# Every engine's instructions in the order of the framework's finer simulation in place of its simple one

## The chip, the cores and the metric

The kernel runs on one core of a Trainium2 chip. A core has five engines with a queue of instructions each: TensorE (PE, matrix products), VectorE (DVE), ScalarE (ACT), GpSimd (POOL) and SyncE (SP, which here only issues transfers). An engine takes its instructions in the order in which they stand in its queue, and they wait for each other across engines by semaphores. The metric is the device time of one execution in microseconds, as a median of runs.

## The reference, cut to what matters

Two networks of two layers each, one behind the other, on 512 tokens of width 1024, in float32. The first also has 256 context tokens:

```
first_block:  per layer
  h = modulate(rms_norm(x), shift, scale)     # from c: w_mod, w_ada
  a = mla_attend(...)       # 8 heads, latent queries and keys
  b = diff_attend(...)      # 4 heads: softmax(q1 k1) - lam * softmax(q2 k2)
  x = x + gate * (merge of a and b) @ w_out
  x = x + gate * conv_ffn(modulate(rms_norm(x)))      # hidden width 2816
second_block:  per layer
  m = even_mixer(rms_norm(x))   # layer 0: pooling and a gated unit
  m = odd_mixer(rms_norm(x))    # layer 1: sparse attention (compressed,
                                #   selected, window keys) and retention
  x = x + rms_norm(m)
  x = x + rms_norm(swiglu(rms_norm(x)))
```

## The kernel before, in words

Activations lie with the 1024 features on partitions, as eight tiles of 128 x tokens (512, or 768 with the context). Every float32 weight tile of 128 x 1024 is loaded by SP into `wraw` (L286), and split into a high part `whi` (ACT, L295) and the rest `wlo` (DVE, L296). Activations `u` are split the same way (L319 to L324). A product is three matmuls: high by high, high by low, low by high (`mm` L330, `prods` L425). There are three buffers each for `wraw`, `whi` and `wlo`.

A norm runs over several engines: squares on ACT (L496), sums of tiles on DVE or POOL (L498), column sums on PE (L509, L586), scale and epsilon on DVE (L342), the power -1/2 on POOL (L343), and a broadcast over partitions on PE (`rowcast`, L349). What uses the broadcast differs by place: L1431/L1433 at startup, L1247/L1250 in the first network, L1604/L1605 and L324 in the second.

The modulation vectors of a layer come from 32 blocks of `w_ada` (`araw`, 512 KB each, L524). For each block and each of the two conditions DVE multiplies and sums (L537) and adds a bias (L538):

```
nc.vector.tensor_scalar(v[:, :n], sums, scale, eps, ...)           # L342
nc.gpsimd.tensor_tensor(r, v[:, :n], self.mhalf[:, :n], op=ALU.pow) # L343
nc.vector.scalar_tensor_tensor(self.junk, raw, 0.5, self.silu[cnd],
                       op0=ALU.mult, op1=ALU.mult, accum_out=m)     # L537
```

In the differential heads a score unit is four matmuls into one `psJ` (L751); its maximum is DVE's L778, its exponential ACT's L769. Then PE transposes the probabilities (L684) and multiplies them by the values. In the sparse attention, keys and values of blocks are summed into compressed ones: DVE builds `cmpx` (L1914), ACT and DVE split it into `cmpp` (L1918, L1919), PE multiplies it by the compression weights (L1927).

Two things set the order. The code issues work interleaved by hand: `weave` (L1048) and `beside` (L435) step several generators by pace numbers in the table `W`, and `ahead_by` raises the priority of some instructions. Then the framework's scheduler, in the `TileContext` of L2410, simulates the engines and puts on each engine's queue, in turn, the instruction that is ready and has the highest priority in that simulation. Priorities follow the order of the code.

## Time and profile before

| | us |
|---|---|
| median of three runs | 3378.22 |
| range | 3376.92 to 3384.22 |
| the profiled execution | 3375.24 |
| its span | 3373.4 |
| PE busy in it | 3266.5 (97%) |
| DVE busy | 2249.4 (67%) |
| ACT busy | 1386.3 (41%) |
| POOL busy | 491.6 (15%) |

Busy is the time in which an engine has an instruction in work; a PE that is busy can still run at the lower of its two clocks. The chain of work that ended last is PE for 45% of the span, DVE 4%, ACT 2% and POOL 1%. TensorE's granted clock is 0.8 to 0.9 of full speed in the first of the 40 slices and near full behind it.

### The profile page before, as it was taken

What the parts mean: (1) busy time and instruction counts of PE and PEld (TensorE: products, weight loads), DVE (VectorE), ACT (ScalarE), POOL (GpSimd) and SP (SyncE); (2) the same over time, 40 slices, a digit from 0 to 9 for tenths busy, and PEclk for the clock granted to TensorE, in tenths of its full rate; (3) what the DMA queues carried; (4) which work ended last, traced back from release to release, by engine and by line L of the source; (5) the groups of instructions that cost most, each with busy time, mean ns of one, the idle gap of its engine ahead of it and who ended that gap; (6) DMA issues with size and microseconds to landing.
All of it is one profiled execution on the core that took longest, in us unless ns stands there. A gap on an engine that the chain in (4) does not pass through costs nothing.

```text
span 3373.4 us, 45291 instructions
## 1 busy us (share of the span) xinstructions
PE 3266.5 (97%) x17605; PEld 2777.2 (82%) x17605; DVE 2249.4 (67%) x3822; ACT 1386.3 (41%) x2389; POOL 491.6 (15%) x490
## 2 busy tenths in 40 slices
PE   7999999999999999998999999999999989999998
PEld 4888878888888887887788888888888877798887
DVE  7958788468775565667866656777555777764555
ACT  5236566233222243545734333454232435552222
POOL 2002133210000011112330000221000513420001
PEclk8999999999999999999999999999999999999999
DMA  8721113323442121221162223222323231222222
GB/s 301 261 80 34 54 35 114 130 74 126 162 163 88 63 100 60 91 75 35 48 210 82 96 98 106 77 97 79 103 94 112 84 105 45 91 94 88 95 99 75
DMA packets 106567, 339.43 MB, mean 101 GB/s; under 512 B 12592, under 2 KB 18096, under 8 KB 106352
## 3 DMA queue, kind: packets, MB, share of 16 engines
q1 hardware_dynamic: 97920, 314.38, 27.8%
q0 software_dynamic: 3248, 11.67, 0.9%
q10 hardware_dynamic: 5184, 10.49, 0.8%
q8 instruction: 138, 2.26, 0.3%
q14 instruction: 77, 0.63, 0.1%
HBM read 312.24 MB, written 24.25 MB: 100 GB/s over the span
## 4 chain that ended last, share of the span: by engine, by line
PE 45%; DVE 4%; ACT 2%; issue 2%; POOL 1%; DMA 0%; ACTq 0%; POOLq 0%; DVEq 0%; SPq 0%
PE psM L425 38%; PE psM L330 2%; PE psJ L974 1%; DVE u L324 1%; PE psM L1032 1%; PE psM L2125 1%; PE psM L2086 1%; DVE wlo L296 0%; PE psM L684 0%; DVE t L1605 0%; PE psM L2117 0%; DVE t L1604 0%; PE psM L509 0%; POOL sm L343 0%; POOL stat L498 0%
## 5 line engine op out<-in xcount | busy, mean ns | idle before, releaser
L425 PE MATMUL psM<-u,whi 128*128 128x512 f32 (+1 forms) x5312 | 1434.6, 362 | 2.5 <-ACT u L322 1.0
L425 PEld LDWEIGHTS psM<-u,whi 128*128 128x128 f32 x5312 | 928.0, 189 | 157.3 <-ACT u L322 2.4
L425 PE MATMUL psM<-u,wlo 128*128 128x512 f32 (+1 forms) x2656 | 912.9, 362 | 1.9 <-DVE wlo L296 1.9
L295 ACT ACTIVATE whi<-wraw 128x1024 fp32r<-128x1024 f32 x393 | 413.6, 1054 | 990.0 <-PE psM L425 609.9
L296 DVE TENSOR_TENSOR wlo<-wraw,whi 128x1024 fp32r<-128x1024 f32 x393 | 488.4, 1244 | 279.8 <-ACT whi L295 277.7
L425 PEld LDWEIGHTS psM<-u,wlo 128*128 128x128 f32 x2656 | 481.3, 189 | 78.8 <-DVE wlo L296 2.6
L330 PE MATMUL psM<-u,whi 128*128 128x512 f32 (+1 forms) x1610 | 428.7, 352 | 2.7 <-DVE u L320 1.3
L330 PEld LDWEIGHTS psM<-u,whi 128*128 128x128 f32 x1610 | 280.2, 190 | 45.0 <-issue 2.1
L330 PE MATMUL psM<-u,wlo 128*128 128x512 f32 (+1 forms) x805 | 280.4, 349 | 0.0
L425 PE MATMUL psM<-u,wspare 128*128 128x256 f32 (+1 forms) x1584 | 254.7, 315 | 4.3 <-DVE t L1604 3.2
L425 PE MATMUL psJ<-u,whi 128*128 128x512 f32 (+1 forms) x1184 | 257.6, 337 | 0.0
L425 PEld LDWEIGHTS psM<-u,wspare 128*128 128x128 f32 x1584 | 225.0, 194 | 21.4 <-issue 3.3
L498 POOL TENSOR_TENSOR stat<-stat,t 128x256 f32<-128x256 f32 x100 | 94.7, 961 | 973.3 <-ACT t L496 907.6
L425 PEld LDWEIGHTS psJ<-u,whi 128*128 128x128 f32 x1184 | 181.8, 188 | 27.1
L330 PEld LDWEIGHTS psM<-u,wlo 128*128 128x128 f32 x805 | 152.8, 190 | 20.2 <-DVE wlo L296 0.4
L537 DVE SCALAR_TENSOR_TENSOR silu<-araw,silu 128x1024 f32<-128x1024 f32 x128 | 156.0, 1219 | 16.6 <-DMA araw<-in_w_ada_dram 16.4
L322 ACT ACTIVATE u<-t 128x512 fp32r<-128x512 f32 (+2 forms) x114 | 77.5, 682 | 215.1 <-DVE t L1308 128.3
L425 PE MATMUL psJ<-u,wlo 128*128 128x512 f32 x592 | 154.2, 338 | 0.0
L320 DVE TENSOR_TENSOR pt<-psM,pt 128x512 fp32r<-128x512 f32 x156 | 105.9, 685 | 36.9 <-ACT pt L319 35.3
L319 ACT ACTIVATE pt<-psM 128x512 fp32r<-128x512 f32 x156 | 91.5, 595 | 88.9 <-PE psM L684 83.2
L324 DVE SCALAR_TENSOR_TENSOR u<-t,u 128x512 fp32r<-128x512 f32 (+2 forms) x114 | 88.1, 775 | 49.3 <-ACT u L322 49.2
L330 PE MATMUL psM<-whi,u 128*128 128x512 f32 (+2 forms) x356 | 113.0, 386 | 4.0 <-DVE V L655 2.6
(356 smaller groups left out, 4385.2 us busy)
## 6 DMA issues: line engine op xcount, KB each, us to landing
wraw<-in_w_up_dram SPq DMA_DIRECT2D x88, 512.0 KB, 3.5
wraw<-in_ffn_gu_dram SPq DMA_DIRECT2D x88, 512.0 KB, 3.5
araw<-in_w_ada_dram SPq DMA_DIRECT2D x80, 512.0 KB, 4.3
wraw<-in_w_in_dram SPq DMA_DIRECT2D x70, 512.0 KB, 3.5
wraw<-in_w_down_dram SPq DMA_DIRECT2D x44, 512.0 KB, 3.5
wraw<-in_ffn_dn_dram SPq DMA_DIRECT2D x44, 512.0 KB, 3.5
wraw<-in_od_in_dram SPq DMA_DIRECT2D x24, 512.0 KB, 3.5
araw<-in_w_mod_dram SPq DMA_DIRECT2D x16, 512.0 KB, 10.2
```

Source lines behind the costliest of these rows:

```text
L295: nc.scalar.activation(hi[:, :n], raw[:, :n], AF.Copy)
L296: (nc.gpsimd if pool else nc.vector).tensor_sub(lo[:, :n], raw[:, :n], hi[:, :n].bitcast(F32))
L319: nc.scalar.activation(hi, src, AF.Copy)
L320: (nc.gpsimd if pool else nc.vector).tensor_sub(lo, src, hi.bitcast(F32))
L322: nc.scalar.activation(hi, src, AF.Copy, scale=scale) if isinstance(scale, float) else \
L324: nc.vector.scalar_tensor_tensor(lo, src, scale, hi.bitcast(F32), op0=ALU.mult, op1=ALU.subtract)
L330: nc.tensor.matmul(out, w[a][wrows, wcols], x[b][xrows, xcols], start=first and i == 0, stop=last and i == 2)
L425: self.nc.tensor.matmul(ps[:, lo - c0:hi - c0], w[a][:, wc], x[b][:, lo:hi], start=first and i == 0 and a == b, stop=last and i == len(ks) ...
L498: (nc.vector if last == 1 else nc.gpsimd).tensor_add(st["acc"][:, c], st["acc"][:, c], s[:, c])
L537: nc.vector.scalar_tensor_tensor(self.junk, raw, 0.5, self.silu[cnd], op0=ALU.mult, op1=ALU.mult, accum_out=m)
L974: self.nc.tensor.matmul(ps[:, c0 - keys[0][0]:c1 - keys[0][0]], q[:96, x, qs:qs + 128], k[:96, y, c0:c1], start=i == 0, stop=i == 2)
L1032: nc.tensor.matmul(o, V[:, kt, i], pt[:, b], start=kt == 0 and b == 0, stop=kt == 5 and b == 1)
```

## The change

One argument of the context in which the whole kernel is built. With it the scheduler runs its simulation of the engines in the finer form instead of the simple one. The instructions, their tiles and their number stay; what an engine does after what changes, and with it the semaphore waits.

```diff
@@ -2407,7 +2407,7 @@
     io["out"] = nc.dram_tensor("out_0_dram", [KD, 128, T], F32, kind="ExternalOutput").ap()
-    with tile.TileContext(nc) as tc:
+    with tile.TileContext(nc, schedule_with_timeline_sim=True) as tc:
         Build(nc, tc, io).run()
```

Three places show what moves. On DVE at startup, around the norm step of the context's tokens (L342, `sm_515`). `mod00` and `mod10` are the modulation vectors of the two conditions, `araw_663` to `araw_777` blocks of `w_ada`, `t3_488` the running sum of squares. Before:

```order
L581 TENSOR_TENSOR t3_488<-t3_502,t3_488 128x256
L538 TENSOR_TENSOR mod00_74<-mod00_74,c_cols_66 128x1
L537 SCALAR_TENSOR_TENSOR silu_105,mod10_76<-araw_663,silu_107 128x1024
L581 TENSOR_TENSOR t3_488<-t3_505,t3_488 128x256
L538 TENSOR_TENSOR mod10_76<-mod10_76,c_cols_66 128x1
L537 SCALAR_TENSOR_TENSOR silu_105,mod00_74<-araw_700,silu_106 128x1024
L342 TENSOR_SCALAR sm_515<-psM_510 128x2
L538 TENSOR_TENSOR mod00_74<-mod00_74,c_cols_66 128x1
L537 SCALAR_TENSOR_TENSOR silu_105,mod10_76<-araw_700,silu_107 128x1024
L1431 SCALAR_TENSOR_TENSOR t3_568<-t3_132,mods_140,psM_519 128x256
```

After:

```order
L581 TENSOR_TENSOR t3_488<-t3_502,t3_488 128x256
L538 TENSOR_TENSOR mod10_76<-mod10_76,c_cols_66 128x1
L537 SCALAR_TENSOR_TENSOR silu_105,mod00_74<-araw_737,silu_106 128x1024
L581 TENSOR_TENSOR t3_488<-t3_505,t3_488 128x256
L538 TENSOR_TENSOR mod00_74<-mod00_74,c_cols_66 128x1
L537 SCALAR_TENSOR_TENSOR silu_105,mod10_76<-araw_737,silu_107 128x1024
L342 TENSOR_SCALAR sm_515<-psM_510 128x2
L538 TENSOR_TENSOR mod10_76<-mod10_76,c_cols_66 128x1
L537 SCALAR_TENSOR_TENSOR silu_105,mod00_74<-araw_777,silu_106 128x1024
L538 TENSOR_TENSOR mod00_74<-mod00_74,c_cols_66 128x1
L537 SCALAR_TENSOR_TENSOR silu_105,mod10_76<-araw_777,silu_107 128x1024
L1431 SCALAR_TENSOR_TENSOR t3_568<-t3_132,mods_140,psM_519 128x256
```

Three more blocks of `w_ada` stand ahead of L342, and two instead of one between it and the first L1431. On SP's queue the loads of the third and fourth block (`araw_737`, `araw_777`) moved ahead of three weight tiles, those of eight later blocks ahead of the weight tile `wraw_800`, and the rotary tables ahead of `wraw_558`.

On PE in the sparse attention of the second network, where the compression (L1927) begins. `psM_23526` to `psM_23529` are projections. Before:

```order
L330 MATMUL psM_23529<-whi_23532,u4_22598 128x280
L330 MATMUL psM_23529<-wlo_23533,u4_22598 128x280
L330 MATMUL psM_23529<-whi_23532,u4_22598 128x280
L1927 MATMUL psM_23572<-cmpp_23431,whi_23575 128x128
L1927 MATMUL psM_23572<-cmpp_23431,wlo_23576 128x128
L1927 MATMUL psM_23572<-cmpp_23431,whi_23575 128x128
L1927 MATMUL psM_23572<-cmpp_23431,wlo_23576 128x128
L330 MATMUL psM_23526<-whi_23585,u4_22599 128x280
L330 MATMUL psM_23526<-wlo_23586,u4_22599 128x280
```

After:

```order
L330 MATMUL psM_23529<-whi_23635,u4_22603 128x280
L330 MATMUL psM_23529<-wlo_23636,u4_22603 128x280
L330 MATMUL psM_23529<-whi_23635,u4_22603 128x280
L1927 MATMUL psM_23572<-cmpp_23431,whi_23575 128x128
L1927 MATMUL psM_23572<-cmpp_23431,wlo_23576 128x128
L1927 MATMUL psM_23572<-cmpp_23431,whi_23575 128x128
L1927 MATMUL psM_23572<-cmpp_23431,wlo_23576 128x128
```

Sixty matmuls of the projections moved ahead of the first L1927. On DVE the splits of the weights that they use (`wlo_23586`, `wlo_23636`) moved ahead of the two L1919 that make `cmpp_23431` and `cmpp_23432`.

On PE in the first layer's differential heads, at the first score unit (`psJ_2095`); `psM_2111` and `psM_2170` are the next head's projections. Before:

```order
L330 MATMUL psM_2111<-u6_427,wlo_2106 128x512
L330 MATMUL psM_2111<-u6_468,whi_2105 128x512 x2
L751 MATMUL psJ_2095<-u6_2086,u6_2016 128x512
L751 MATMUL psJ_2095<-u6_2086,u6_2016 128x256
L751 MATMUL psJ_2095<-u6_2086,u6_1947 128x512
L751 MATMUL psJ_2095<-u6_2086,u6_1947 128x256
L330 MATMUL psM_2111<-u6_468,wlo_2106 128x512
L751 MATMUL psJ_2115<-u6_2086,u6_2016 128x512
```

After:

```order
L330 MATMUL psM_2170<-u6_422,wlo_2106 128x256
L330 MATMUL psM_2170<-u6_427,whi_2105 128x256
L751 MATMUL psJ_2095<-u6_2086,u6_2016 128x512
L751 MATMUL psJ_2095<-u6_2086,u6_2016 128x256
L751 MATMUL psJ_2095<-u6_2086,u6_1947 128x512
L751 MATMUL psJ_2095<-u6_2086,u6_1947 128x256
L751 MATMUL psJ_2115<-u6_2086,u6_2016 128x512
```

The unit moved behind the rest of `psM_2111` and half of `psM_2170`, and the second unit follows it without a matmul between. In words, at the norm boundaries: near 715 us L342 (`sm_6739`) moved ahead of two L1247 and four L1250, and PE's L349 twelve matmuls forward. Near 2268 us the split `wlo_20156` moved to right behind the first L342, L349 behind 24 instead of four matmuls; the second L342 (`sm_20197`) moved ahead of five L324 and two L498.

## Rows read from the trace of the kernel before

**Rows 1.** The page, part 1: busy us, share of the span, instructions.

```profile
PE 3266.5 (97%) x17605; PEld 2777.2 (82%) x17605; DVE 2249.4 (67%) x3822; ACT 1386.3 (41%) x2389; POOL 491.6 (15%) x490
```

**Rows 2.** Stretches: length, busy us by engine (count), PE clock, DMA share, GB/s.

```profile
84.00:340.00 256.00, 251.11 (x1422) 217.86 (x1421) 201.45 (x413) 106.38 (x207) 25.71 (x18) 1.00 0.36 124
340.00:700.00 360.00, 348.04 (x2040) 297.05 (x2039) 243.30 (x456) 181.48 (x351) 101.81 (x93) 1.00 0.25 84
700.00:1250.00 550.00, 548.28 (x3104) 476.66 (x3103) 380.92 (x620) 168.44 (x220) 9.57 (x10) 1.00 0.34 112
1250.00:1700.00 450.00, 432.49 (x2219) 356.01 (x2218) 310.32 (x567) 233.50 (x429) 94.38 (x88) 0.99 0.21 71
...
2100.00:2330.00 230.00, 220.96 (x1414) 201.11 (x1413) 168.49 (x294) 116.73 (x224) 50.59 (x56) 0.99 0.27 90
...
2600.00:3010.00 410.00, 382.62 (x2286) 327.65 (x2285) 301.83 (x604) 206.78 (x471) 146.10 (x171) 0.97 0.27 88
```

**Rows 3.** Waits of PE: who waited for what, us in total, times, longest.

```profile
PE psM L349 <- POOL sm L343: 10.8, 10, 2.4
...
PE psM L1927 <- DVE cmpp L1919: 4.1, 1, 4.1
PE psJ L751 <- DVE u L743: 3.9, 4, 1.8
...
PE psM L1927 <- ACT whi L295: 1.5, 1, 1.5
...
PE psM L1927 <- DVE wlo L296: 1.4, 2, 0.9
```

**Rows 4.** The page, part 5: groups; busy, mean ns, idle before, releaser.

```profile
L537 DVE SCALAR_TENSOR_TENSOR silu<-araw,silu 128x1024 f32<-128x1024 f32 x128 | 156.0, 1219 | 16.6 <-DMA araw<-in_w_ada_dram 16.4
```

**Rows 5.** Timeline, startup: start, us, instruction; in brackets idle before and releaser.

```profile
69.35 0.16 DVE L342 TENSOR_SCALAR sm<-psM 128x2 f32<-128x2 f32 x1 [2.74 <-PE psM L586]
...
69.59 1.68 POOL L343 TENSOR_TENSOR sm<-sm,mhalf 128x2 f32<-128x2 f32 x1 [19.80 <-DVE sm L342]
...
71.33 0.43 PE L349 MATMUL psM<-c_ident,sm 128*128 128x128 f32 x2 [1.43 <-POOL sm L343]
...
71.80 0.87 DVE L1431 SCALAR_TENSOR_TENSOR t<-t,mods,psM 128x256 f32<-128x256 f32 x2 [1.08 <-PE psM L349]
```

**Rows 6.** Timeline of DVE, 74 to 81 us: the first and the last L1433.

```profile
74.58 0.48 DVE L1433 SCALAR_TENSOR_TENSOR u<-t,mods,u 128x256 fp32r<-128x256 f32 x1 [1.13 <-ACT u L1432]
...
80.13 0.48 DVE L1433 SCALAR_TENSOR_TENSOR u<-t,mods,u 128x256 fp32r<-128x256 f32 x1
```

**Rows 7.** Timeline, norm at 715 us.

```profile
714.63 0.15 DVE L342 TENSOR_SCALAR sm<-psM 128x4 f32<-128x4 f32 x1
...
714.85 2.00 POOL L343 TENSOR_TENSOR sm<-sm,mhalf 128x4 f32<-128x4 f32 x1 [15.42 <-DVE mod L538]
...
716.90 0.54 PE L349 MATMUL psM<-c_ident,sm 128*128 128x128 f32 x3 [1.44 <-POOL sm L343]
```

**Rows 8.** Timeline, first norm at 2268 us.

```profile
2268.96 0.71 POOL L343 TENSOR_TENSOR sm<-sm,mhalf 128x2 f32<-128x2 f32 x1 [0.67 <-DVE sm L342]
...
2269.73 0.43 PE L349 MATMUL psM<-c_ident,sm 128*128 128x128 f32 x2 [0.46 <-POOL sm L343]
```

**Rows 9.** Timeline, second norm at 2284 us.

```profile
2283.15 0.39 PE L425 MATMUL psM<-u,wlo 128*128 128x256 f32 x1 [0.93 <-DVE wlo L296]
...
2283.97 1.62 POOL L343 TENSOR_TENSOR sm<-sm,mhalf 128x2 f32<-128x2 f32 x1 [3.75 <-DVE sm L342]
...
2285.66 0.43 PE L349 MATMUL psM<-c_ident,sm 128*128 128x128 f32 x2 [1.29 <-POOL sm L343]
```

**Rows 10.** Timeline, compression: two L330 in a row and PE's first L1927.

```profile
2703.18 0.29 PE L330 MATMUL psM<-wlo,u 128*128 128x280 f32 x1
...
2703.31 0.28 PE L330 MATMUL psM<-whi,u 128*128 128x280 f32 x1
...
2707.68 0.38 PE L1927 MATMUL psM<-cmpp,whi 128*128 128x128 f32 x1 [4.09 <-DVE cmpp L1919]
```

**Rows 11.** Stretch 2700 to 2740 us, columns as in group two.

```profile
2700.00:2740.00 40.00, 32.10 (x170) 28.70 (x170) 30.01 (x47) 16.16 (x31) 6.33 (x4) 0.83 0.25 84
```

## Prediction

> **What bounds the kernel now.** I read the page first: TensorE (PE) is busy 3266.5 of 3373.4 us [rows 1], so what an order can save is what PE stands idle, 107 us, and what it loses at the lower of its two clocks. Then the table by stretches [rows 2]. The feed-forward stretch from 700 to 1250 us idles 1.7 us in 550 (550 - 548.3). The stretches with attention and norms hold the idle time: 4.9 us in 84 to 340, 12.0 in 340 to 700, 17.5 in 1250 to 1700, 9.0 in 2100 to 2330 and 27.4 in 2600 to 3010. Third the list of what PE waits for [rows 3]: many small waits, led by the broadcast of a norm's factor (L349) behind GpSimd's power (L343), 10.8 us in ten waits. Last the timeline at the places where the two orders differ most. In the feed-forward stretches they differ by a few rows, so no term comes from there.
>
> The profiled execution took 3375.24 us, span 3373.4. The sum is made against that; the median of the runs is 3 us higher, and I add these 3 us at the end.
>
> **What the change does, part by part.** It adds, removes and resizes no instruction. Each engine runs its own queue in order, so an instruction that is not ready holds everything behind it. The price of a new order is therefore the waits that it makes less the waits that it takes away.
>
> *Startup, 57 to 95 us: later.* VectorE (DVE) forms the modulation vectors in blocks of 1.22 us (L537 [rows 4]), which nobody needs soon. Before, three of them stand ahead of L342, the norm step that PE's broadcast waits for, and one between L342 and the first L1431. Now six and two stand there, and twelve instead of four ahead of the last L1433, which finishes the context's tokens. Step by step: three more blocks ahead of L342 at 1.22 us and a little addition each are 3.9 us. DVE stood idle 2.74 us ahead of L342 [rows 5], so L342 goes from 69.35 to about 70.7. GpSimd's L343 and PE's L349 [rows 5] follow by 1.4 us. Up to the last L1433 the eight extra blocks are 10.4 us, of which the idle 2.74 + 1.08 + 1.13 us in front of L342, L1431 and L1433 [rows 5, 6] take 4.95. So that L1433 is some 5.5 us late, at 86 instead of 80.1 [rows 6]. PE needs it and the weights' low halves (L296) that stand behind it on DVE. Other matmuls of the new order cover a part and the next splits cost again: I take +5 us, between 0 (all covered) and +10.4 (nothing covered, no idle time used). On SyncE's queue loads of those blocks and the rotary tables stand ahead of weight loads. The weights concerned are split late anyway, so I cost that at nothing; without that cover it is in the slower rival.
>
> *Norm at 715 us: earlier.* L342 stood behind six L1247/L1250 steps and now stands ahead of two L1247 and four L1250. Each is about 0.4 us, so it starts some 2 us earlier than 714.63 [rows 7]. PE's L349 stands 12 matmuls earlier. Its wait of 1.44 us goes: -1.5, between 0 and -1.7.
>
> *Norms at 2268 to 2286 us, and the same again at 2984 to 3001.* The split that PE waited for at 2283.15 (0.93 us [rows 9]) now stands right behind the first L342, 13 us earlier. The first L349 stands 24 matmuls behind the sums instead of 4, so the 0.46 us wait goes [rows 8]. The second L342 is ahead of five L324 and two sums instead of behind; PE wants its result 4 us earlier than before. Of the 1.29 us [rows 9] I let 0.4 stand. That is 0.93 + 0.46 + 0.9 = 2.3 us a place and -4.6 for two, between 0 and -5.4.
>
> The rows show what sits beside L343 on DVE. With a block L537 or a split L296 beside it, L343 takes 1.68, 2.00 and 1.62 us [rows 5, 7, 9]; alone 0.71 [rows 8]. By that mechanism L343 is 1 us shorter at 715, where L1247 now follows, and 0.9 longer at 2268 and 2984, where the moved split follows. The longer ones are covered by the 20 matmuls put ahead of L349 (2.4 us), so the sum stands. The Trainium skill, "SBUF — State Buffer", section "Who interferes with whom", says a DVE instruction with two inputs in SBUF contends with GpSimd reading SBUF. By that rule the change pays about 0.9 us twice if the cover fails, and my -4.6 would be -2.8; these rows agree with the rule.
>
> *Compression in the sparse attention, 2700 to 2740 us: earlier.* PE had four L1927 at the head of its queue and waited 4.09 us for DVE's L1919 [rows 10]. Sixty of the projection matmuls (L330) that stood behind them are now ahead, and 32 L1927 follow in one block. Two of them start 0.13 us apart [rows 10], so that is 8 us of work. DVE, in turn, does the splits for those projections and the rotary steps first. Walking DVE's rows at their traced lengths puts the first L1919 at about 2713, and PE arrives at about 2711.5, so 1.5 of the 4.1 us stand. The other L1927 waits are 1.5 and 1.4 us [rows 3]. PE idles 7.9 us in this stretch, and its granted clock is 0.83 on average, so between the levels of 1.2 and 2.4 GHz [rows 11]. At 0.83 a third of the 40 us runs at the half level, which costs at most 6.8 us more. So the bounds are 0 and -14.7; I take -5, 2.6 of the first wait and most of the two smaller ones, and none of the clock.
>
> *The weave inside attention.* In the differential heads the first score unit (L751) stood at once behind its inputs and PE waited for them; now 17 and more projection matmuls stand ahead, so the 3.9 us in four waits [rows 3] can go. Elsewhere score units that stood apart now stand in pairs and fours, and the projections in longer runs. The latent heads' values and scores start 10 us earlier in the first layer. What this gives I can't walk through. The idle time of the four attention stretches outside the places above is 4.9 + 12.0 + 17.5 + 19.5 (27.4 less 7.9) = 53.9 us, so the lower end is -54. The upper end is as much again as 340 to 700 idles now, +12. I take -6, near the only row that clearly goes.
>
> Sum: +5 - 1.5 - 4.6 - 5 - 6 = -12.1; 3375.2 - 12.1 = 3363.1, and with the 3 us 3366.
>
> **The rivals.**
>
> *No change that can be seen* (3371 to 3385). Small waits move, and each one gone brings the next forward: the entry of the second block at 2126 to 2160 keeps its ten sums on GpSimd whatever the order. For it: the feed-forward stretches don't move and the terms are each under 8 us. Against it: the 4.09 us wait stands behind work that was ready. It gives 3378. Chance 0.22.
>
> *Slower: the modulation blocks hold DVE at startup.* DVE already lost 16.4 us to blocks whose loads hadn't landed [rows 4]. If the blocks now pulled ahead reach DVE before their loads land, then everything behind them (norm factor, split weights) waits, and PE after it. The price is the full 10.4 us of extra blocks plus about as much as half of those 16.4, some 18 us. It decides from the point where a block's load lands after L342 could have started. With a third of my gains (-6) it gives 3378 + 18 - 6 = 3390. For it: PE has no other work there. Against it: the loads concerned are issued earlier too. Chance 0.23.
>
> *Much faster.* If the finer order takes half of the 54 us in attention, not a tenth: 3366 - 21 = 3345. For it: all the waits there are for results that were nearly ready. Against it: long runs of projections use up the work that could cover later softmax steps. Chance 0.12.
>
> **How the numbers follow.** My forecast has 0.43: 3366, with its own range of 3352 to 3372. A difference of 0.2%, 6.8 us, is about what a measurement of this kernel can tell from no change; faster means under 3371.4, slower over 3385. Faster is 0.43 + 0.12 = 0.55, same 0.22, slower 0.23. For eight in ten the range reaches from the much faster case to just past the slower one: 3338 to 3392.
>
> **What would show it.** In the changed profile PE should wait under 2 us for L1919; the L349 waits should fall from 10.8 to about 6 us; the windows 2600 to 3010 and 1250 to 1700 should idle less, and 0 to 100 us about 5 us more, with L342 near 70.7. I am wrong if PE's idle time in the attention stretches grows: then the pairs and long runs matter, which I didn't cost. If L537 waits for its loads, the slower rival holds.

## The result, and the profile after

The changed kernel is slower. Its median is 3462.4 us (3458.1 to 3464.0, four runs) against 3379.8 us of the kernel before in the same session (3376.9 to 3384.2, four runs); the ratio is 1.0243, 95% interval 1.0231 to 1.0255, so +83 us. Forecast were 3366 us, with a range that ended at 3392. None of the rivals was it: the slower one has another place, and its price of 18 us is a fifth of this.

First the page of the changed kernel, part 1, which answers to [rows 1].

```profile
PE 3292.2 (95%) x17605; PEld 2800.9 (81%) x17605; DVE 2246.9 (65%) x3822; ACT 1379.8 (40%) x2389; POOL 486.7 (14%) x490
```

The span grew by 82.9 us (3456.3 against 3373.4). Of this, 57 are idle time of PE (164.1 against 106.9), and 26 are busy time of PE with the same 17,605 matmuls. Most of that is time at the lower clock (mean granted 0.982 against 0.989); some 4 us of it lie in a feed-forward stretch whose granted clock is 1.00 (last section). The other engines have the same work. Next the table by stretches, at the places that answer to [rows 2].

```profile
87.00:366.00 279.00, 258.00 (x1408) 221.68 (x1408) 198.70 (x389) 108.37 (x209) 25.08 (x18) 0.98 0.31 104
366.00:725.00 359.00, 345.27 (x2041) 297.07 (x2040) 242.37 (x455) 179.74 (x351) 101.64 (x93) 1.00 0.25 83
725.00:1280.00 555.00, 553.32 (x3106) 479.77 (x3106) 379.02 (x621) 168.53 (x220) 8.22 (x10) 1.00 0.35 111
1280.00:1750.00 470.00, 433.66 (x2211) 358.13 (x2210) 308.66 (x564) 231.69 (x429) 94.13 (x87) 0.98 0.20 66
2153.00:2387.00 234.00, 221.35 (x1414) 201.60 (x1413) 169.25 (x296) 116.11 (x225) 51.72 (x56) 0.98 0.28 89
2656.00:3089.00 433.00, 393.30 (x2295) 337.12 (x2294) 303.06 (x605) 205.06 (x469) 142.67 (x168) 0.95 0.26 84
```

PE's idle time (length less busy time) went from 4.9 to 21.0 us in the first piece, from 17.5 to 36.3 in the fourth and from 27.4 to 39.7 in the last. The feed-forward piece still idles 1.7. So the loss lies in the attention stretches, where the forecast had a gain. Matmul by matmul it can be placed: at points where both kernels have finished the same set of matmuls, I took the changed kernel's time less that of before. The delay grows as follows (us of the kernel before).

| stretch | forecast | measured |
|---|---|---|
| start to 207 | +5 | +3.1 |
| 207 to 374, differential heads, layer 0 | weave | +22.5 |
| 374 to 684, latent heads, layer 0 | weave | -1.2 |
| 684 to 759, norm at 715 | -1.5 | +0.7 |
| 759 to 1246, feed-forward | 0 | +4.3 |
| 1246 to 1432, lead-in and heads, layer 1 | weave | +2.7 |
| 1432 to 1714, heads, layer 1 | weave | +18.8 |
| 1714 to 2237, with a norm at 1780 | 0 | +2.8 |
| 2237 to 2614, norm at 2268 | -2.3 | +3.9 |
| 2614 to 2787, compression | -5 | -0.5 |
| 2787 to 2931, sparse attention | weave | +20.4 |
| 2931 to 3047, norm at 2984 | -2.3 | +2.0 |
| 3047 to the end | 0 | +2.8 |

The five rows of the weave make +63.2; forecast was -6. Small rows are to be read with care. Eight kernels of the experiments below (e2, e3, e5, e6, e7, e9, e10, e15) have the order of before from 2787 to 2931 us, and in their traces that stretch still takes 2.8 to 3.0 us longer; in e4 it is 0.0. So a row of under 3 us can't be put down to the order by this table alone. The waits of PE in the changed kernel, which answer to [rows 3]:

```profile
PE psM L330 <- DVE V L655: 11.8, 4, 3.8
PE psM L425 <- DVE u L324: 10.2, 4, 6.5
PE psJ L974 <- ACT t L988: 10.1, 13, 1.3
...
PE psM L349 <- POOL sm L343: 6.1, 4, 2.4
...
PE psJ L751 <- ACT t L769: 2.5, 4, 1.0
...
PE psM L1927 <- DVE cmpp L1919: 0.7, 1, 0.7
PE psJ L751 <- DVE u L743: 0.6, 2, 0.3
```

The waits that the forecast wanted gone are gone: L349 10.8 to 6.1, L1919 4.1 to 0.7, the scores' wait for L743 3.9 to 0.6. Others, longer, have come: values split late (L655), a normalized tile split late (L324), an exponential (L988).

**What happens in the differential heads.** The rows below show PE, ACT and DVE of the changed kernel, in this order, around the first score units (start, us, instruction, idle before).

```profile
253.30 1.57 PE L751 MATMUL psJ<-u,u 128*128 128x512 f32 x8
...
261.62 0.85 PE L751 MATMUL psJ<-u,u 128*128 128x512 f32 x4
...
256.31 0.90 ACT L769 ACTIVATE t<-psJ,sm 128x768 f32<-128x768 f32 x1 [6.46 <-DVE sm L779]
...
263.76 0.90 ACT L769 ACTIVATE t<-psJ,sm 128x768 f32<-128x768 f32 x1 [4.62 <-DVE sm L779]
...
262.51 0.96 DVE L778 TENSOR_REDUCE sm<-psJ 128x1 f32<-128x768 f32 x1 [1.57 <-PE psJ L751]
...
279.78 0.72 DVE L719 STREAM_SHUFFLE t<-psM 128x512 f32<-128x512 f32 x1
```

And the same in the kernel before.

```profile
242.17 0.98 PE L751 MATMUL psJ<-u,u 128*128 128x512 f32 x4 [0.61 <-DVE u L743]
...
246.50 0.98 PE L751 MATMUL psJ<-u,u 128*128 128x512 f32 x4
...
245.46 0.90 ACT L769 ACTIVATE t<-psJ,sm 128x768 f32<-128x768 f32 x1 [3.66 <-DVE sm L779]
...
264.88 0.74 DVE L719 STREAM_SHUFFLE t<-psM 128x512 f32<-128x512 f32 x1
```

Score units use two buffers `psJ` in turn. Before, the first exponential ends at 246.36 and frees the first buffer; PE starts the third score unit at 246.50. After, it ends at 257.21, and PE starts the third at 261.62: for 4.4 us the buffer and the inputs are there and PE runs projections that stand ahead in its queue. No wait of PE shows it. It shows as idle time of the others. ACT waits 4.62 us for DVE at the third unit, 2.23 before. From 231 to 271 us PE is busy 40.0 of 40 us and DVE 23.0; before, in the 40 us from 225, they were 37.9 and 31.8. The single wait of DVE for the third score is no longer than before (1.57 against 2.09 us), but over the stretch such waits (us in total, times, longest) grow from

```profile
DVE sm L778 <- PE psJ L751: 5.9, 8, 2.1
```

to

```profile
DVE sm L778 <- PE psJ L751: 9.5, 12, 3.2
```

Then it comes back. The next head's first step after the projection of its keys (the shuffle L719) stands on DVE behind this head's softmax steps. Its projection was finished at 262.7 us against 261.0 before, but L719 comes at 279.78 instead of 264.88, and the next head's scores wait for it. The end of the split L743 that opens the first and the fourth head shows the pace, before:

```profile
241.16 1.94 DVE L743 TENSOR_TENSOR u<-t,u 64x768 fp32r<-64x768 f32 x2
...
337.27 0.95 DVE L743 TENSOR_TENSOR u<-t,u 64x768 fp32r<-64x768 f32 x1 [0.36 <-ACT u L742]
```

and after:

```profile
249.07 1.94 DVE L743 TENSOR_TENSOR u<-t,u 64x768 fp32r<-64x768 f32 x2
...
361.91 1.94 DVE L743 TENSOR_TENSOR u<-t,u 64x768 fp32r<-64x768 f32 x2
```

Three heads take 95.1 us before (243.10 to 338.22) and 112.8 after (251.01 to 363.85). The projections run early are missing later: PE idles 15 us more in the stretch.

### The profile page after: what moved, and what is told of

The parts are those of the page before. It is cut to its first block, busy times and chain, and to the rows that moved or that the text cites. A ratio compares the mean times of both kernels' runs of the same rounds, so it can differ in the third digit from the quotient of the medians.

```text
span 3456.3 us, 45365 instructions
## 1 busy us (share of the span) xinstructions
PE 3292.2 (95%) x17605; PEld 2800.9 (81%) x17605; DVE 2246.9 (65%) x3822; ACT 1379.8 (40%) x2389; POOL 486.7 (14%) x490
## 4 chain that ended last, share of the span: by engine, by line
PE 84%; DVE 9%; ACT 3%; issue 2%; POOL 1%; DMA 0%; DVEq 0%; ACTq 0%; POOLq 0%
PE psM L425 49%; PE psM L330 16%; PE psJ L425 9%; PE psJ L974 2%; DVE wlo L296 1%; PE psM L684 1%; PE psJ L751 1%; PE psM L1032 1%; PE psJ L330 1%; DVE u L320 1%; ACT whi L295 1%; DVE pt L320 0%; DVE t L1604 0%; DVE sm L986 0%; PE psM L2086 0%
## 5 line engine op out<-in xcount | busy, mean ns | idle before, releaser
L296 DVE TENSOR_TENSOR wlo<-wraw,whi 128x1024 fp32r<-128x1024 f32 x393 | 491.3, 1252 | 288.2 <-ACT whi L295 285.7
L330 PE MATMUL psM<-u,whi 128*128 128x512 f32 (+1 forms) x1610 | 432.7, 356 | 17.0 <-DVE V L655 6.1
L330 PEld LDWEIGHTS psM<-u,whi 128*128 128x128 f32 x1610 | 285.5, 193 | 60.0 <-issue 11.0
L330 PE MATMUL psM<-u,wlo 128*128 128x512 f32 (+1 forms) x805 | 283.6, 353 | 0.0
L498 POOL TENSOR_TENSOR stat<-stat,t 128x256 f32<-128x256 f32 x100 | 102.5, 1042 | 994.4 <-ACT t L496 925.8
L330 PEld LDWEIGHTS psM<-u,wlo 128*128 128x128 f32 x805 | 155.1, 193 | 21.0 <-DVE wlo L296 0.2
L330 PE MATMUL psM<-whi,u 128*128 128x512 f32 (+2 forms) x356 | 112.0, 386 | 7.1 <-DVE V L655 5.7
L324 DVE SCALAR_TENSOR_TENSOR u<-t,u 128x512 fp32r<-128x512 f32 (+2 forms) x114 | 86.4, 762 | 36.1 <-ACT u L322 35.9
```

Of the source, the lines that this page charges most:

```text
L296: (nc.gpsimd if pool else nc.vector).tensor_sub(lo[:, :n], raw[:, :n], hi[:, :n].bitcast(F32))
L324: nc.vector.scalar_tensor_tensor(lo, src, scale, hi.bitcast(F32), op0=ALU.mult, op1=ALU.subtract)
L330: nc.tensor.matmul(out, w[a][wrows, wcols], x[b][xrows, xcols], start=first and i == 0, stop=last and i == 2)
L498: (nc.vector if last == 1 else nc.gpsimd).tensor_add(st["acc"][:, c], st["acc"][:, c], s[:, c])
```

## The experiments

The theory: each engine takes its queue in order, so the time depends on where the attention matmuls stand among the projections on PE, and the new order puts them too late (PE theory). Its rivals: the startup; the queues of the vector engines; something else that the other simulation sets, such as buffers and semaphores. All but e12 use pieces of the two orders that exist. A table of places is added to the kernel, and what it lists is pinned one behind the other on its engine by order edges, which only fix the order within that engine; what is not listed ("free") is put in place by the simulation of the base kernel. What the pinning itself costs was not measured by pinning the order of before unchanged; e8 at +2.4 us and e14 at +5 have most of that order pinned, and e12 is faster than the kernel before.

```diff
     with tile.TileContext(nc) as tc:
         Build(nc, tc, io).run()
+        _fixed_order(nc, tc)
...
+def _fixed_order(nc, tc):
+    traced = list(nc.cur_bb.bb.instructions)
+    for steps in json.loads(zlib.decompress(base64.b85decode(_ORDER))):
...
+                tc.add_manual_dep(traced[k], traced[prev].name, mybir.DependencyInfo(mybir.DependencyClass.NoSync, mybir.DependencyReason.DATA), reason="order")
```

Below, each diff says which order the table holds. Medians stand against the kernel before in the same session (3376.9 to 3381.3).

**e1: the order alone.**

```diff
-all engines: order of before
+all engines: order of the changed kernel (simple simulation)
```

> The simple simulation builds the kernel, but every engine's instructions are pinned one behind the other in the order of the changed kernel. If the order alone makes the loss, the time is that of the changed kernel, 3462 us (3455 to 3468), and PE's idle time is about 164 us. If something else that the finer simulation sets (which semaphores are waited for, which buffers the tiles get) makes it, the time stays nearer to the kernel before, under 3440 us.

3471.6 us, ratio 1.0278 (1.0256 to 1.0299). The order alone makes the loss; it is even 12 us more than the changed kernel lost, a little past what was expected. The order is the same on every engine, but the program has nine more instructions that only handle semaphores. What makes these 12 us is open.

**e2 and e3: where.**

```diff
-all engines: order of before
+e2: 200 to 370 us as in the changed kernel, the rest as before
+e3: 200 to 370, 1440 to 1720, 2770 to 2935 us as before, the rest as in the changed kernel
```

> The order of the changed kernel only from 200 to 370 us (the differential heads of layer 0, on all engines), the order of before ahead of it and behind it. Place theory: the loss belongs to the stretch in which it shows, so +23 us over the kernel before (20 to 26), that is about 3403 us. Rival, startup: the modulation blocks and their loads moved at the start shift what comes later, so this kernel, whose start is that of before, loses under 8 us.

> The reverse: the order of the changed kernel everywhere but in three attention stretches (200 to 370, 1440 to 1720 and 2770 to 2935 us of the kernel before), which have the order of before. Place theory: 23 + 19 + 20 us of the loss of 83 us are gone, so about 3400 us (3393 to 3412), some +20 us over the kernel before. Rival, startup or clock spread over the whole run: under half of the loss comes back, over 3420 us.

e2: 3400.4 us, +23.5, ratio 1.0067 (1.0049 to 1.0085), as the place theory has it. e3: 3414.5 us, +37.5, ratio 1.0106 (1.0087 to 1.0125). Of e1's 94.6 us 57 come back, more than half, but 5 us less than the 62 expected and 2 us outside the range that was given. The rest of e3 is many small losses: in its trace +6 at startup, +8 from 1240 to 1440 us, +5 at the norm at 2268.

**e4 to e7: which engine, and what on it** (200 to 370 us, elsewhere the order of before).

```diff
-200 to 370 us: all engines as before
+e4: PE as in the changed kernel, the others free (simple simulation)
+e5: PE as before, the others free (finer simulation)
+e6: as e4, but L751 at its places of before among the projections
+e7: as e4, but all matmuls that are no projections at their places of before
```

> The order of before, but from 200 to 370 us PE alone is pinned to the order of the changed kernel, and the other four engines are ordered around it by the simple simulation. PE theory (PE runs projections while attention matmuls stand ready behind them): +16 to +26 us over the kernel before, nearly all that e2 loses. Rival, vector queues (VectorE and ScalarE take the steps of the next head too late): with these queues free the loss is under 8 us.

> The reverse of e4: from 200 to 370 us PE alone is pinned to the order of before, and the other four engines are ordered around it by the finer simulation; the rest of the program has the order of before. PE theory: little is lost, 0 to +8 us over the kernel before. Rival, the other queues: +12 us and more.

> As e4 (PE in the order of the changed kernel from 200 to 370 us, the others free), but each of the 40 score products (L751) is put back to the place among the projection matmuls that it has in the kernel before. If the late scores alone make the loss, +0 to +8 us over the kernel before. If the later links of a head (transposes and products with the values) are held up as much, most of e4's loss stays, +12 to +20 us.

> As e6, but every matmul that is not a projection (scores, transposes, products with the values) is put back to its place among the projections of the kernel before; the projections keep the order of the changed kernel. PE theory, in the form that what counts is where the attention matmuls stand among the projections: +0 to +8 us over the kernel before. Rival, the order of the projections themselves and of their weights: +15 us or more.

| | median us | over before | ratio |
|---|---|---|---|
| e4 | 3401.0 | +24.1 | 1.0066 (1.0048 to 1.0084) |
| e5 | 3387.3 | +8.2 | 1.0025 (1.0016 to 1.0034) |
| e6 | 3403.7 | +24.5 | 1.0070 (1.0051 to 1.0089) |
| e7 | 3387.7 | +8.6 | 1.0023 (1.0012 to 1.0033) |

PE's order alone, with the other engines ordered around it, costs all that e2 costs, and with PE's old order two thirds of it are gone. e5 and e7 lie just past the +8 us that were expected, and what makes their 8 us is open. The stretch in the traces of before, of the changed kernel (which comes to it 3 us later), of e4 and of e7, one fence each (columns as in the table by stretches):

```profile
203.00:370.00 167.00, 161.64 (x914) 138.35 (x913) 128.47 (x259) 93.34 (x189) 30.35 (x22) 1.00 0.13 45
```

```profile
206.00:396.00 190.00, 169.64 (x918) 143.82 (x917) 133.74 (x258) 92.94 (x189) 29.83 (x22) 0.96 0.12 39
```

```profile
203.00:392.00 189.00, 171.55 (x921) 146.07 (x921) 134.07 (x257) 92.66 (x189) 30.00 (x22) 0.95 0.11 40
```

```profile
203.00:377.00 174.00, 165.44 (x917) 141.04 (x916) 130.13 (x257) 93.32 (x189) 30.86 (x22) 0.98 0.13 43
```

The idle time goes from 5.4 to 20.4 and 17.5 us, and back to 8.6 in e7. PE's busy time goes with it, 161.6 to 169.6 and 171.6 us for nearly the same matmuls, while the granted clock falls from 1.00 to 0.96 and 0.95 on average, so some matmuls run at 1.2 GHz instead of 2.4. A third of the changed kernel's loss in the stretch (8 of 23 us) is this, and 10 of 22 in e4. One fall in the changed kernel, the piece ahead of it and the piece at the lower clock:

```profile
265.00:279.40 14.40, 11.48 (x62) 9.31 (x61) 12.13 (x24) 9.70 (x17) 2.58 (x2) 1.00 0.12 37
```

```profile
279.50:286.00 6.50, 5.49 (x25) 5.49 (x26) 6.11 (x12) 2.94 (x11) 3.15 (x2) 0.50 0.00 0
```

PE stood idle for 2.9 of the 14.4 us ahead of the fall. In these four traces the clock goes with the gaps, and in e7, where most of the gaps are gone, it is at 0.98. So the loss of clock follows from the order; that it is the gaps that bring it down is read off these rows, and no run sets the one without the other.

e6 was a surprise in size, above the +12 to +20 us of its second case: with the scores alone put back nothing is won. PE's waits in e6, then in e7:

```profile
PE psM L330 <- ACT pt L319: 8.7, 7, 2.4
PE psJ L751 <- ACT t L769: 2.9, 5, 1.3
```

```profile
PE psM L330 <- ACT pt L319: 2.9, 2, 2.6
```

In e6 the wait only moves down the chain: PE waits 8.7 us for the transposed probabilities (`pt`), since transposes and products with the values still stand where the changed kernel puts them. In e7 all links are back and most of the loss is gone. So what counts is where the whole chain stands among the projections. Their own order is hardly a rival here: by line, tile name and shape, the 378 projection matmuls of the stretch stand in the same sequence in the traces of before, of the changed kernel, of e4 and of e7. Which link alone would do was not tried.

**e8: the same in the sparse attention.**

```diff
-2770 to 2935 us: all engines as before
+2770 to 2935 us: PE's projections as in the changed kernel, its other matmuls at their places of before, the others free
```

> The same as e7 in the NSA attention, 2770 to 2935 us: PE has the projections in the order of the changed kernel and the attention matmuls at their places of the kernel before, the other engines are free, the rest of the program is that of before. In the changed kernel this stretch loses 18 us. PE theory: +0 to +8 us over the kernel before. Rival, the queues of VectorE and ScalarE decide here: +12 us or more.

3381.6 us, +2.4, ratio 1.0009 (0.9999 to 1.0019), where the changed kernel loses 20 (NSA is the sparse attention). This is as the PE theory has it, but from one side only: PE's new order alone was not run here, so for this stretch the cause is not shown.

**e9 and e10: the heads of layer 1.**

```diff
-1440 to 1720 us: all engines as before
+e9: PE as in the changed kernel, the others free (simple simulation)
+e10: PE as before, the others free (finer simulation)
```

> As e4, in the second stretch that loses: from 1440 to 1720 us (the end of the differential heads and the latent-attention heads of layer 1) PE alone is pinned to the order of the changed kernel, the other engines are ordered around it by the simple simulation, the rest is the order of before. The changed kernel loses 19 us there. PE theory: +14 to +24 us over the kernel before. Rival, the other queues decide in this stretch: under +8 us.

> The reverse of e9, as e5: from 1440 to 1720 us PE is pinned to the order of before, the other engines are ordered around it by the finer simulation. PE theory: 0 to +8 us over the kernel before. If the other queues carry a loss of their own here, +10 us or more.

e9: 3409.3 us, +32, ratio 1.0092 (1.0075 to 1.0109), more than was expected and than the changed kernel itself loses there. e10: 3395.9 us, +19, ratio 1.0057 (1.0042 to 1.0072). The PE theory fails here: PE's new order loses, but with PE's old order the other engines' new order also loses as much as the changed kernel does there. PE's longest waits in e10, 1440 to 1740 us:

```profile
PE psM L684 <- POOL t L990: 7.2, 7, 1.9
PE psM L330 <- DVE u L320: 3.9, 1, 3.9
```

The first was 3.2 us in five waits before. Now the steps that PE wants next stand late on the other engines.

**e11, e13 and e14: which other engine** (the whole program; base is the changed kernel).

```diff
-all engines: finer simulation
+e11: PE as before, the rest free (finer simulation)
+e13: PE and DVE as before, the rest free
+e14: PE, DVE and ACT as before, POOL and SP free
```

> PE pinned to the order of before in the whole program, the other four engines ordered by the finer simulation around it. If PE's order alone makes the loss of the changed kernel, the time is within 20 us of the kernel before (under 3400 us). If the finer simulation misplaces steps on the other engines as well (V's evictions, the norms, the blocks at the start), which PE in its fixed order then meets one by one, it is 3420 us and more.

> PE and VectorE pinned to the order of before in the whole program, the other three engines ordered by the finer simulation around them. If the loss of e11 (PE alone pinned, +97 us) is made by VectorE's order under PE's, most of it goes: +20 to +45 us over the kernel before. If ScalarE, GpSimd or the loads make it, +60 us and more stay.

> PE, VectorE and ScalarE pinned to the order of before, only GpSimd and SyncE (the loads) ordered by the finer simulation. If the order of the three that pass tiles to each other is what counts, 0 to +12 us over the kernel before; if the loads or GpSimd's steps count, over +20 us.

| | median us | over before | ratio |
|---|---|---|---|
| e11 | 3474.4 | +97 | 1.0284 (1.0267 to 1.0301) |
| e13 | 3408.0 | +27 | 1.0070 (1.0053 to 1.0087) |
| e14 | 3386.3 | +5 | 1.0016 (1.0006 to 1.0025) |

With PE in its old order everywhere the kernel is no faster than the changed one (+97 against +83). DVE in its old order as well takes 70 us away, ACT 22 more; what the simulation does with GpSimd and the loads is worth 5. PE's waits in e11 are at other places than in the changed kernel:

```profile
PE psM L2125 <- ACT u L319: 10.4, 6, 6.3
PE psM L425 <- DVE u L324: 9.5, 8, 2.1
PE psM L330 <- DVE u L320: 9.0, 5, 3.9
PE psM L1927 <- DVE cmpp L1919: 9.0, 1, 9.0
```

The wait for L1919, forecast to shrink, is twice that of [rows 3] here: DVE does other things first, and PE in its old order has no projections to do meanwhile. So there is not one bad queue. The likely reading is that the orders of PE, DVE and ACT, which come from one simulation, fit each other, and where one engine keeps its old order and the others get new ones, PE meets each late step singly; e11, e13 and e14 fit it, but don't show it step by step. (DVE's order in e11 is the one that the simulation makes around PE's old order, so not quite that of the changed kernel.)

**e15: a norm forecast to gain.**

```diff
-all engines: order of before
+2236 to 2342 us as in the changed kernel, the rest as before
```

> The order of before, with that of the changed kernel only from 2236 to 2342 us (the norm behind the attention merge of layer 1 and the lead-in of what follows). Forecast of the prediction for this place: about -2 us. The delay that the changed kernel gains there: +4 us. Expected: +2 to +6 us over the kernel before if the place loses by its own order, about 0 if the loss comes in from further up.

3386.1 us, +4.8, ratio 1.0016 (1.0006 to 1.0025): the place loses by its own order. PE's waits there in e15:

```profile
PE psM L425 <- ACT u L322: 2.3, 1, 2.3
PE psM L425 <- DVE u L324: 1.3, 1, 1.3
PE psM L425 <- ACT u L323: 1.3, 1, 1.3
```

The waits for L343 and for the split (1.8 and 0.9 us before, in this stretch) are gone as forecast. In their place PE waits 4.9 us for the normalized tiles' splits, where before those were 1.7.

**e12: small moves on the order of before.** Two of the 749 changed places, on DVE and on PE at the norm at 2284 us:

```diff
+L342 TENSOR_SCALAR sm_20197<-psM_20192 128x2
 L324 SCALAR_TENSOR_TENSOR u4_19813<-t2_15659,c_cols_66,u4_19813 128x256
...
-L342 TENSOR_SCALAR sm_20197<-psM_20192 128x2
...
+L425 MATMUL psM_20142<-u4_19812,wspare_19849 128x256
+L425 MATMUL psM_20142<-u4_19812,wspare_19849 128x256
 L349 MATMUL psM_20446<-c_ident_68,rc_19816 128x128
```

> The order of before with 749 of its 24,453 places changed, from 205 us on, by small moves: a block of 1 to 16 neighbours on one engine goes up to 32 places earlier or later, taken where an in-order replay of the durations measured in the two traces ends sooner. Theory: what counts is whether, at each place, a projection stands ready where PE would wait; if the replay holds every wait that matters, this is 20 to 30 us faster than the kernel before (3350 to 3360 us). Rival: such waits of under 1 us each are refilled by others, or depend on semaphores and the clock, which the replay leaves out; then it is within 8 us of the kernel before.

3364.3 us, ratio 0.9962 (0.9947 to 0.9977), so 13 us (8 to 18) faster than before: half of what was expected, between the two theories. This version beats both kernels. Its order was chosen by the durations that the traces of this chip show, and it leaves the chains of before together. PE's idle time in its trace is 100.6 us (3364.9 less 3264.3) against 106.9, which is 6.3 of the 8.5 us that the two traces differ by. Its waits for L343 are 8.0 us against 10.8:

```profile
PE psM L349 <- POOL sm L343: 8.0, 7, 2.4
```

## Why the prediction was wrong

**The step that failed** is "The weave inside attention": "What this gives I can't walk through ... I take -6". It measured +63. The prediction saw the rows that matter ("now 17 and more projection matmuls stand ahead", "score units that stood apart now stand in pairs and fours, and the projections in longer runs") and priced only the wait that they remove, 3.9 us. It did not ask who waits for the score. Its bounds were made from PE's idle time: -54, and +12 "as much again as 340 to 700 idles now". A stretch that idles 5 us can lose 22: idle time bounds what can be won, not what can be lost. Nor did it count the clock on top. What the runs showed in its place differs by stretch. In the heads of layer 0 the attention matmuls stand too late among the projections on PE (e4 +24 us, with their old places +9 in e7). In the heads of layer 1 PE's new order and the other engines' new order each lose alone (e9 +32, e10 +19). In the sparse attention the old places of the attention matmuls on PE bring the time back (e8 +2.4 us), and no more is known.

The argument that would have done it stands in the last rival, where it was used against a gain only: "long runs of projections use up the work that could cover later softmax steps". As a slower rival it was missing.

**Startup** (+5): +3.1. The sign was right and the mechanism in part. L342 came at 69.10 instead of 70.7. DVE's idle 2.74 us were used up, as reckoned, but two of the three weight splits (L296, 1.2 us each) that stood among these steps before are no longer there, which the prediction left out. L343 took 1.68 us as before [rows 5]. The last L1433 began at 83.6 us, 3.5 later than before, where 5.5 were forecast:

```profile
69.10 0.16 DVE L342 TENSOR_SCALAR sm<-psM 128x2 f32<-128x2 f32 x1
```

The slower rival did not come. It said that the blocks would wait for their loads, and over the whole kernel these waits did double, to 34.0 us against 16.4 [rows 4]:

```profile
L537 DVE SCALAR_TENSOR_TENSOR silu<-araw,silu 128x1024 f32<-128x1024 f32 x128 | 156.2, 1220 | 34.1 <-DMA araw<-in_w_ada_dram 34.0
```

But none of them is at startup: in both traces all of them lie behind 700 us. So the rival priced its case from a row that belongs to another place, and PE has no waits there that follow from them.

**Norm at 715 us** (-1.5): +0.7 over the piece from 684 to 759 us. Its steps held. GpSimd's L343 is 1.0 us shorter (1.01 against 2.00), as the prediction had it, and PE no longer waits for it [rows 7]:

```profile
737.71 1.01 POOL L343 TENSOR_TENSOR sm<-sm,mhalf 128x4 f32<-128x4 f32 x1 [13.88 <-DVE sm L342]
...
738.93 0.60 PE L349 MATMUL psM<-c_ident,sm 128*128 128x128 f32 x4
```

The changed kernel's delay falls by 1.5 us at this place, as forecast, and is back some 4 us later, where PE waits 1.1 us for the next normalized tiles (L1250, L1249), 0.3 before.

**Norms at 2268 and 2984 us** (-4.6 for both): +3.9, which e15 bears out, and +2.0, which may be chance. The waits named [rows 8, 9] are gone, and the question "what is late next" was not asked: the splits of the normalized tiles (e15). L343, forecast 0.9 us longer at the first of the two norms, took 0.71 us as before, and 0.89 instead of 1.62 at the second. At the first the moved split began on DVE 0.4 us behind L343 and ran beside its last 0.3 us only; at the second DVE ran L324, which has two inputs in SBUF too, all through the 0.89 us. So the price that the prediction took from the rule of the Trainium skill ("SBUF — State Buffer", "Who interferes with whom") did not come, and the first norm hardly tests the rule; the loss is elsewhere.

**Compression** (-5): -0.5. The wait for L1919 fell to 0.7 us (1.5 were forecast). But the weights of the projections put ahead were themselves late, which the prediction had counted as split in time:

```profile
2766.88 0.40 PE L330 MATMUL psM<-wlo,u 128*128 128x280 f32 x1 [3.40 <-DVE wlo L296]
...
2776.53 0.40 PE L330 MATMUL psM<-wlo,u 128*128 128x280 f32 x1 [3.20 <-DVE wlo L296]
...
2781.11 0.48 PE L1927 MATMUL psM<-cmpp,whi 128*128 128x128 f32 x1 [0.72 <-DVE cmpp L1919]
```

4.1 us of waiting [rows 10] became 3.40 + 3.20 + 0.72.

What the prediction named as its own refutation did occur: PE's idle time in the attention stretches grew. Open is why the finer simulation puts the projections ahead; no run shows what it takes each step to last.

## What to carry to other kernels

A queue taken in order hides its damage: while PE runs projections ahead of a ready score, it shows no wait, and the loss stands as idle time of DVE and ACT, and a head later as PE's. When an order changes, look for each chain that goes round (score, softmax, next head's first step, next score) at how long its links stand behind other work with their inputs ready, and bound the loss by that, not by the idle time that is there now. Orders of several engines belong together: taking the good order for one engine alone (e11) won nothing.

## What the runs showed of the hardware that was not expected

From 844 to 964 us of the kernel before and from 869 to 991 of the changed one, PE is never idle, its granted clock is 1.00, and it does the same kind of feed-forward matmuls; yet it takes 2 us longer for only two matmuls more, of some 0.17 us each. Before, then after:

```profile
844.00:964.00 120.00, 120.00 (x694) 104.92 (x693) 89.80 (x155) 31.65 (x39) 0.00 (x0) 1.00 0.46 156
```

```profile
869.00:991.00 122.00, 122.00 (x696) 106.08 (x695) 90.45 (x157) 32.76 (x40) 0.00 (x0) 1.00 0.47 151
```

Over the piece from 759 to 1246 us this makes 4.3 us, and in the traces of the other kernels between about -2 and +9. Nine of them (e2, e4 to e10, e15) have the order of before in this piece, and still differ from the kernel before by -1.9 to +1.9 us there, so the order in the piece does not make those. The cause is open.
